# A state space layer on one Trainium2 core: how its input reaches the products for the states

## The chip, the core and the metric

The program runs on one core of one Trainium2 chip. The metric is the device time of one execution in microseconds (us), less being better. The engines of a core run side by side, each through a queue of its own in program order: TensorE (PE; its weight loads stand as PEld), VectorE (DVE), ScalarE (ACT), GpSimd (POOL) and SyncE (SP). SP computes nothing; here it issues the loads of the weights. ACT and POOL issue some transfers too.

## The reference, cut to what matters

Three blocks of a language model run one after the other on 256 places with 1024 features. The third block has a state space layer (`s5_mixer`), in which 32 groups of 16 inputs each drive 64 complex states:

```python
bu = jnp.einsum('bsgh,gph->bsgp', uf.astype(jnp.complex64), b_bar)
a = jnp.broadcast_to(lam_bar, bu.shape)
_, states = lax.associative_scan(combine, (a, bu), axis=1)
y = jnp.einsum('bsgp,ghp->bsgh', states, c).real + d_skip * uf
```

Beside it stand a short convolution and an attention with q, k and v; then an output projection and a feed-forward layer.

## The kernel before

All weights are read as 32-bit numbers and used as a high and a low part. A feeder (`Feeder`, lines 35 to 117) does this: SP loads a chunk into one of three buffers `raw` (line 61), ACT writes the high part `wh` (line 72), DVE the low part `wl` (line 86), and TensorE multiplies high by high, high by low and low by high. As soon as a chunk is split, SP is given the load that takes its buffer. Six units (half a chunk each, mostly) may be split ahead of their use. Since every engine works in program order, a unit's `wl` on DVE also stands behind whatever was issued to DVE before it.

The third block is `block2` (lines 1169 to 1359). Its order around the change:

1. `enter` makes q. The generator `s5` is then started (line 1210): POOL issues three loads, `bT`, `cT` and `dT`, from DRAM, where earlier code has left prepared matrices (line 824).
2. `fm_pair` multiplies for the first half of u (two of the four blocks of 128 features); `put_u(0)` scales it on DVE (line 1206) into `uT`, which is laid out as [128 features, block, i, k] for place 4k + i. The next `fm_pair` and `put_u(1)` do the second half.
3. A further `fm_pair` makes kv. With `tick` the generator `s5` is taken one step on, and from here it is stepped between the other products: after kv, after ks, after kw, and then in `conv_in`, in whose steps the generator `heads` (norms and transposes of q and k) takes part too.

A step J of the loop at line 887 calls `outputs(J - 2)` and then `states(J)`. There are 32 groups, 8 in each block J; two groups share one set of 128 rows of states, so a block has four sets of 32 features (jj). Four consecutive places (i) are taken together, so a step in time is four places long, and 64 such steps (k) remain for the scan.

`states(J)` (line 837) needs, for each set jj, the product of 32 features by four places with 128 states, real and imaginary (e). Before the change a product always spans all 128 rows of features. To keep the four sets apart, POOL first writes `um` (`masked`, line 830): four copies of the block of u, each with three quarters of its rows set to zero by the mask `rows4`. One product (line 842) then has 256 columns (four sets of 64), and four of them, one for each i, are added up. `masked(0)` is made by POOL right after `put_u(0)`; `masked(J + 1)` stands behind the products of block J, since there is one buffer. After the products ACT copies the sums to `bu` (line 847), and POOL (lines 852, 853, 864, 865) and DVE (lines 854 to 869) rotate, scan and rotate back.

`outputs(J)` (line 872) multiplies `uT` and the states with `dT` and `cT` and writes back over `uT`.

In the lists of instructions each of the products in 32-bit numbers stands as two matmuls.

Of the kernel before, what the change touches and what calls it, by code (L numbers as in the profile page):

```python
# [9 lines left out]
F32 = _mybir.dt.float32  # L10
# [4 lines left out]
OP = _mybir.AluOpType  # L15
# [130 lines left out]
class Net:  # L146
# [669 lines left out]
    def s5(self, p, uT, sp):  # L816

        nc = self.nc
        V, G, A, PE = nc.vector, nc.gpsimd, nc.scalar, nc.tensor
        bT = sp.tile([128, 4, 2, 4, 128], F32, name="bT")  # L820
        cT = sp.tile([128, 4, 2, 4, 128], F32, name="cT")
        dT = sp.tile([128, 4, 4, 128], F32, name="dT")
        for t, src in zip((bT, cT, dT), p["dram"]):
            G.dma_start(t, src)
        yield

        def t4(name, bufs=1):
            return sp.tile([128, 4, 64], F32, tag=name, bufs=bufs, name=name)

        def masked(J):  # L830
            um = sp.tile([128, 4, 4, 64], F32, tag="um", bufs=1, name="um")
            u2 = um.rearrange("p b i k -> p b (i k)")
            G.tensor_tensor(u2, uT[:, J].rearrange("p i k -> p (i k)")[:, None, :].to_broadcast([128, 4, S]),
                            self.rows4[:, :, None].to_broadcast([128, 4, S]), op=OP.mult)
            return um

        def states(J):

            ps = self.tr()
            for e in range(2):  # L840
                for i in range(4):
                    PE.matmul(ps[:, e * 256:e * 256 + 256], bT[:, 3 - i, e, J, :], um[0][:, :, i, :],  # L842
                              start=i == 0, stop=i == 3)
            if J < 3:
                um[0] = masked(J + 1)
            bu = sp.tile([128, 2, 4, 64], F32, tag="bu", bufs=1, name="bu")
            A.activation(bu.rearrange("p e j t -> p (e j t)"), ps, AF.Copy)
            c, s = p["sc"][:, 0, 4 * J:4 * J + 4, :], p["sc"][:, 1, 4 * J:4 * J + 4, :]
            br, bi = bu[:, 0], bu[:, 1]

            t1, t2, t3, t4_ = t4("t1"), t4("t2"), t4("t3"), t4("t4")
            G.tensor_tensor(t3, bi, c, op=OP.mult)
            G.tensor_tensor(t4_, br, s, op=OP.mult)
            V.tensor_tensor(t1, br, c, op=OP.mult)
            V.tensor_tensor(t2, bi, s, op=OP.mult)
            V.tensor_tensor(t1, t1, t2, op=OP.add)
            V.tensor_tensor(t3, t3, t4_, op=OP.subtract)
            for g in (t1, t3):
                for jj in range(4):
                    m = p["m4"][:, 4 * J + jj:4 * J + jj + 1].to_broadcast([128, 64])  # L860
                    V.tensor_tensor_scan(g[:, jj, :], m, g[:, jj, :], 0.0, op0=OP.mult, op1=OP.add)
            gr, gi = t1, t3
            hr, hi, t5, t6 = t4("hr", 2), t4("hi", 2), t4("t2"), t4("t4")
            G.tensor_tensor(hi, gr, s, op=OP.mult)
            G.tensor_tensor(t6, gi, c, op=OP.mult)
            V.tensor_tensor(hr, gr, c, op=OP.mult)
            V.tensor_tensor(t5, gi, s, op=OP.mult)
            V.tensor_tensor(hr, hr, t5, op=OP.subtract)
            V.tensor_tensor(hi, hi, t6, op=OP.add)
            return hr, hi  # L870

        def outputs(J, h):
            ps = self.tr()
            for lag in range(4):
                PE.matmul(ps[:, lag * 64:256], dT[:, lag, J, :], uT[:, J, 0:4 - lag, :].rearrange("p i k -> p (i k)"),
                          start=lag == 0, stop=False)
            for i in range(4):
                for jj in range(4):
                    sl = slice(32 * jj, 32 * jj + 32)
                    for e in range(2):  # L880
                        PE.matmul(ps[sl, i * 64 + 1:i * 64 + 64], cT[:, i, e, J, sl], h[e][:, jj, :63],
                                  start=False, stop=i == 3 and e == 1, tile_position=(0, 32 * jj))
            A.activation(uT[:, J].rearrange("p i k -> p (i k)"), ps[:, :S], AF.Copy)
        um = [masked(0)]
        yield
        h = {}
        for J in range(6):
            if J > 1:
                outputs(J - 2, h.pop(J - 2))
            if J < 4:  # L890
                h[J] = states(J)
            yield
# [276 lines left out]
    def block2(self, p, next_g):  # L1169
# [23 lines left out]
        with ExitStack() as ctx:  # L1193
# [6 lines left out]
            with ExitStack() as inner:  # L1200
                s5 = self.s5(p, uT, pool("s5", inner))

                def put_u(o, ps):

                    for a in range(2):
                        V.tensor_tensor(uT[:, 2 * o + a].rearrange("p i k -> p k i"),
                                        r3(ps)[:, a].rearrange("p (k i) -> p k i", i=4),
                                        self.rb.rearrange("p (k i) -> p k i", i=4), op=OP.mult)
                pq = self.enter(next_g)
                next(s5)  # L1210
                d["q"], d["qq"] = [], []
                for t in range(2):
                    q = self.act.tile([128, D], F32, tag="xs", bufs=2, name="q")
                    A.activation(q[:, :512], pq[t], AF.Copy, scale=self.r[:, t:t + 1])
                    d["qq"].append(q)
                    d["q"].append(q[:, :512])
                heads = self.heads(p, d, bp)
                ps = fm_pair()
                self.bcast_r()
                next(heads)  # L1220
                put_u(0, ps)
                put_u(1, fm_pair())
                next(s5)
                ps = fm_pair()
                kv = bp.tile([128, 2, S], F32, name="kv")
                self.times_r(kv.rearrange("p a t -> p (a t)"), ps)
                d["kv"] = [kv[:, i, :] for i in range(2)]
                background.append(s5)
                tick()

                def keys(name, n):
                    pk = [self.mm() for _ in range(2)]
                    self.tm([q[:, :n] for q in pk], x, KT)
                    out = []
                    for t in range(2):
                        k = bp.tile([128, n], F32, name="%s%d" % (name, t))
                        A.activation(k, pk[t][:, :n], AF.Copy, scale=self.r[:, t:t + 1])
                        out.append(k)
                    return out
                ks = keys("ks", 256)  # L1240
                tick()
                kw = keys("kw", 280)
                for name, k in (("s", ks), ("w", kw)):
                    d["k" + name] = [q[:, 0:128] for q in k]
                    d["v" + name] = [q[:, 128:256] for q in k]
                d["gates"] = [q[:, 256:280] for q in kw]
                tick()
                next(heads)
                background.append(heads)

                rb2 = bp.tile([128, S], F32, name="rb2")
                V.tensor_tensor(rb2, self.rb, self.rb, op=OP.mult)

                def conv_in(n):
                    cx = ring()
                    V.tensor_tensor(r3(cx), r3(fm_pair()), rb2[:, None, :].to_broadcast([128, 2, S]), op=OP.mult)
                    tick(n)
                    V.tensor_tensor(cx, cx, fm_pair(), op=OP.mult)
                    tick(n)
                    pb = fm_pair()  # L1260
                    tick(n)
                    return cx, pb
                cx, pb = conv_in(1)
                for g in (s5, heads):
                    for _ in g:
                        pass
                background.clear()
# [158 lines left out]
    def consts2(self):  # L1426
# [9 lines left out]
        for h in range(2):  # L1436
# [16 lines left out]

        self.both = c.tile([32, 16], F32, name="both")
        G.tensor_tensor(self.both, self.ident[0:32, 0:16], self.ident[0:32, 16:32], op=OP.add)

        self.rows4 = c.tile([128, 4], F32, name="rows4")
        G.memset(self.rows4, 1.0)
        G.affine_select(self.rows4, self.rows4, pattern=[[-32, 4]], compare_op=OP.is_ge, fill=0.0, base=0,
                        channel_multiplier=1)  # L1460
        G.affine_select(self.rows4, self.rows4, pattern=[[32, 4]], compare_op=OP.is_ge, fill=0.0, base=31,
                        channel_multiplier=-1)
        self.cmask = c.tile([128, 2, 8], F32, name="cmask")
        G.memset(self.cmask, 0.0)
        G.affine_select(self.cmask, self.cmask, pattern=[[128, 2], [-32, 8]], compare_op=OP.is_ge, fill=-1e30,
# [403 lines left out]
```

## Time and profile before

| | |
|---|---|
| median of 3 runs | 1514.34 us (1512.48 to 1516.26) |
| the profiled execution | 1515.93 us, its span 1514.2 us |
| TensorE busy | 1455.3 us, 96% of the span |
| VectorE busy | 1058.6 us, 70% |
| ScalarE busy | 803.9 us, 53% |
| GpSimd busy | 223.4 us, 15% |
| mean granted clock of TensorE | 0.982 |

The span goes from the first to the last instruction of the program on the core. Lines such as L86 are lines of the kernel. A row of a timeline gives start, duration, engine, line, operation, what is written and read, shapes, the count of merged instructions, and in brackets how long the engine sat idle before and what ended it. The end of a matmul is modelled, so a busy TensorE may still have room. [...]

### The profile page before, as it was taken

Reading aid. Unit: us, or ns where it says so; the run is one execution under the profiler, and the core shown is the slowest. Engines: PE = TensorE matmul, PEld = TensorE weight load, DVE = VectorE, ACT = ScalarE, POOL = GpSimd, SP = SyncE. Lnnn points to the kernel's source line nnn. Section 1 sums busy time; section 2 is a strip of 40 time slices with the busy share of each in tenths; the row PEclk is TensorE's granted clock in tenths of the full one; section 3 lists DMA queues with packets and bytes.
Section 4 is the critical chain, followed back from the end, with each engine's and each line's share of the span. In section 5 each row is a group of like instructions: output and inputs, shape, how many; then the busy total and the mean of one; then the engine's idle time right before and its main releaser. Section 6 shows DMA issues by size and latency. Waiting matters only on the chain.

```text
span 1514.2 us, 23224 instructions
## 1 busy us (share of the span) xinstructions
PE 1455.3 (96%) x9185; PEld 1289.3 (85%) x9185; DVE 1058.6 (70%) x1776; ACT 803.9 (53%) x1319; POOL 223.4 (15%) x267
## 2 busy tenths in 40 slices
PE   8999997899999999999889998999999999999999
PEld 7888887878888888888887997889898899888887
DVE  6777476877774777746687778757976656677753
ACT  6665357566554556545756434545355544465541
POOL 1200000000000040000000455601426444000000
PEclk9999999899999999999989999999999999999999
DMA  8656643346555575564443836767345445555562
GB/s 291 189 176 204 205 139 113 124 132 217 194 181 198 167 236 168 185 217 130 125 137 104 261 119 211 235 223 256 109 130 182 126 135 186 167 188 189 180 208 70
DMA packets 212893, 265.27 MB, mean 175 GB/s; under 512 B 6120, under 2 KB 175568, under 8 KB 212400
## 3 DMA queue, kind: packets, MB, share of 16 engines
q1 hardware_dynamic: 208224, 250.64, 51.0%
q0 software_dynamic: 3232, 9.86, 2.0%
q10 hardware_dynamic: 1328, 3.29, 0.6%
q8 instruction: 72, 1.18, 0.3%
q14 instruction: 37, 0.30, 0.1%
HBM read 257.47 MB, written 6.29 MB: 174 GB/s over the span
## 4 chain that ended last, share of the span: by engine, by line
PE 72%; DVE 16%; ACT 6%; issue 4%; POOL 1%; DMA 1%; SPq 0%; ACTq 0%; DVEq 0%; POOLq 0%
PE mm L201 25%; PE mm L187 17%; PE mm L185 10%; DVE wl L86 5%; PE mm L164 5%; PE mm L166 5%; PE mm L165 5%; PE mm L184 2%; ACT wh L72 2%; DVE xc L1407 1%; ACT xx L341 1%; DVE xx L343 1%; POOL wl L86 0%; DVE bw L755 0%; PE tr L842 0%
## 5 line engine op out<-in xcount | busy, mean ns | idle before, releaser
L86 DVE TENSOR_TENSOR wl<-raw,wh 128x1024 fp32r<-128x1024 f32 (+1 forms) x441 | 546.3, 1252 | 263.2 <-ACT wh L72 260.1
L72 ACT ACTIVATE wh<-raw 128x1024 fp32r<-128x1024 f32 (+2 forms) x472 | 483.2, 1048 | 174.6 <-PE mm L201 112.8
L187 PE MATMUL mm<-xx,wh 128*128 128x512 f32 x1120 | 399.1, 396 | 0.0
L185 PE MATMUL mm<-xx,wl 128*128 128x256 f32 x1280 | 330.7, 279 | 0.0
L164 PE MATMUL mm<-xx,wh 128*128 128x256 f32 x864 | 253.2, 293 | 2.9 <-ACT wh L72 2.9
L185 PEld LDWEIGHTS mm<-xx,wl 128*128 128x128 f32 x1280 | 241.2, 188 | 13.8
L166 PE MATMUL mm<-xx,wl 128*128 128x256 f32 x864 | 249.4, 289 | 2.4 <-DVE wl L86 2.4
L165 PE MATMUL mm<-xx,wh 128*128 128x256 f32 x864 | 249.1, 288 | 0.0
L187 PEld LDWEIGHTS mm<-xx,wh 128*128 128x128 f32 x1120 | 210.1, 188 | 43.2
L164 PEld LDWEIGHTS mm<-xx,wh 128*128 128x128 f32 x864 | 171.1, 198 | 4.0 <-ACT wh L72 3.3
L166 PEld LDWEIGHTS mm<-xx,wl 128*128 128x128 f32 x864 | 170.4, 197 | 3.1 <-DVE wl L86 3.1
L165 PEld LDWEIGHTS mm<-xx,wh 128*128 128x128 f32 x864 | 170.7, 198 | 0.3
L201 PE MATMUL mm<-wl,hh 128*128 128x512 f32 x440 | 137.7, 394 | 0.0
L201 PE MATMUL mm<-wh,hh 128*128 128x512 f32 x440 | 137.3, 393 | 0.0
L201 PE MATMUL mm<-wh,hl 128*128 128x512 f32 x440 | 137.3, 393 | 0.0
L201 PEld LDWEIGHTS mm<-wl,hh 128*128 128x128 f32 x440 | 82.7, 188 | 18.7
L201 PEld LDWEIGHTS mm<-wh,hl 128*128 128x128 f32 x440 | 82.7, 188 | 18.5
L201 PEld LDWEIGHTS mm<-wh,hh 128*128 128x128 f32 x440 | 82.3, 188 | 18.8
L201 PE MATMUL mm<-wh,xx 128*128 128x512 f32 (+3 forms) x384 | 93.7, 377 | 0.3 <-DVE xx L343 0.3
L86 POOL TENSOR_TENSOR wl<-raw,wh 128x1024 fp32r<-128x1024 f32 x31 | 78.1, 2534 | 80.5 <-ACT wh L72 80.5
L585 ACT ACTIVATE sg<-sg 128x512 f32<-128x512 f32 x50 | 31.6, 632 | 107.4 <-DVE sg L419 107.4
L201 PEld LDWEIGHTS mm<-wh,xx 128*128 128x128 f32 x384 | 70.2, 194 | 12.2 <-DVE xx L343 1.2
(674 smaller groups left out, 1913.5 us busy)
## 6 DMA issues: line engine op xcount, KB each, us to landing
raw<-ffn_w_gu SPq DMA_DIRECT2D x80, 1024.0 KB, 5.2
raw<-ffn_w_down SPq DMA_DIRECT2D x50, 1024.0 KB, 5.1
raw<-w_in SPq DMA_DIRECT2D x24, 1024.0 KB, 5.1
raw<-ffn_w_gate_up SPq DMA_DIRECT2D x20, 1024.0 KB, 5.1
raw<-mix_w_in SPq DMA_DIRECT2D x10, 1024.0 KB, 5.5
raw<-mix_w_out SPq DMA_DIRECT2D x8, 1024.0 KB, 4.9
raw<-ffn_w_gu SPq DMA_DIRECT2D x14, 512.0 KB, 5.1
raw<-ffn_w_down SPq DMA_DIRECT2D x10, 512.0 KB, 3.7
```

Of the source, the lines that this page charges most:

```text
L72: nc.scalar.activation(h, raw, AF.Copy)
L86: v.tensor_tensor(l, raw, h.bitcast(F32), op=OP.subtract)
L164: mm(ps, a[0], b[0], start=start, stop=False)
L165: mm(ps, a[0], b[1], start=False, stop=False)
L166: mm(ps, a[1], b[0], start=False, stop=stop)
L184: nc.tensor.matmul(p, wh[:, k, :], self.xx[:, k, :], start=True, stop=False)
L185: nc.tensor.matmul(p[:, :S], wl[:, k, :], self.xh[:, k, :], start=False, stop=False)
L187: nc.tensor.matmul(p, wh[:, k, :], self.xx[:, k, :], start=False, stop=k == nk - 1)
L201: self.nc.tensor.matmul(ps, x[a][:, k, ts], w[b][:, i, :], start=k == 0 and a + b == 0, stop=k == nk - 1 and b == 1)
L341: nc.scalar.activation(self.xh[:, k, ts], p, AF.Copy, scale=g[:, k:k + 1])
L343: nc.vector.scalar_tensor_tensor(self.xl[:, k, ts], p, g[:, k:k + 1], self.xh[:, k, ts].bitcast(F32), op0=OP.mult, op1=OP.subtract)
L585: nc.scalar.activation(sg, sg, AF.Silu)
```

## The change

`masked`, `um` and the mask `rows4` go. The contraction of a product for the states now spans 32 features of one set and the four places i at once: `u4` holds in rows 32i to 32i + 31 the features of set jj at places 4k + i. So a product has 64 columns, needs no adding up, and there are again eight of them in a block. `u4` is brought into this order by SP: for each half of u, 16 transfers from SBUF to SBUF, each of 32 rows with two pieces of 64 numbers (16 KB). `bT` is loaded to match, in four transfers of 32 rows instead of one of 128. The 16 transfers of a half are issued by a step of the generator right after the `put_u` of that half, so one more step stands behind `put_u(0)`.

```diff
         bT = sp.tile([128, 4, 2, 4, 128], F32, name="bT")
+        u4 = sp.tile([128, 4, 4, 64], F32, name="u4")
...
-        for t, src in zip((bT, cT, dT), p["dram"]):
+        for i in range(4):
+            G.dma_start(bT[32 * i:32 * i + 32].rearrange("f j e J n -> f j (e J n)"),
+                        p["dram"][0][:, 3 - i].rearrange("(j f) e J n -> f j (e J n)", j=4))
+        for t, src in zip((cT, dT), p["dram"][1:]):
             G.dma_start(t, src)
         yield
+        for o in range(2):
+            for i in range(4):
+                for jj in range(4):
+                    nc.sync.dma_start(u4[32 * i:32 * i + 32, 2 * o:2 * o + 2, jj, :],
+                                      uT[32 * jj:32 * jj + 32, 2 * o:2 * o + 2, i, :])
+            yield
...
-        def masked(J):
-            um = sp.tile([128, 4, 4, 64], F32, tag="um", bufs=1, name="um")
-            u2 = um.rearrange("p b i k -> p b (i k)")
-            G.tensor_tensor(u2, uT[:, J].rearrange("p i k -> p (i k)")[:, None, :].to_broadcast([128, 4, S]),
-                            self.rows4[:, :, None].to_broadcast([128, 4, S]), op=OP.mult)
-            return um
...
             ps = self.tr()
             for e in range(2):
-                for i in range(4):
-                    PE.matmul(ps[:, e * 256:e * 256 + 256], bT[:, 3 - i, e, J, :], um[0][:, :, i, :],
-                              start=i == 0, stop=i == 3)
-            if J < 3:
-                um[0] = masked(J + 1)
+                for jj in range(4):
+                    c = e * 256 + jj * 64
+                    PE.matmul(ps[:, c:c + 64], bT[:, jj, e, J, :], u4[:, J, jj, :], start=True, stop=True)
...
-        um = [masked(0)]
-        yield
         h = {}
...
                 put_u(0, ps)
+                next(s5)
                 put_u(1, fm_pair())
                 next(s5)
...
-        self.rows4 = c.tile([128, 4], F32, name="rows4")
-        G.memset(self.rows4, 1.0)
-        G.affine_select(self.rows4, self.rows4, pattern=[[-32, 4]], compare_op=OP.is_ge, fill=0.0, base=0,
-                        channel_multiplier=1)
-        G.affine_select(self.rows4, self.rows4, pattern=[[32, 4]], compare_op=OP.is_ge, fill=0.0, base=31,
-                        channel_multiplier=-1)
```

## Rows read from the trace of the kernel before

**Rows 1.** The page: the chain that ended last, by engine

```profile
PE 72%; DVE 16%; ACT 6%; issue 4%; POOL 1%; DMA 1%; SPq 0%; ACTq 0%; DVEq 0%; POOLq 0%
```

**Rows 2.** Stretches of 4 us: busy time (instructions) of PE, PEld, DVE, ACT, POOL; clock; DMA

```profile
1048.00:1052.00 4.00, 4.00 (x35) 4.00 (x34) 2.80 (x5) 3.89 (x7) 0.00 (x0) 1.00 0.53 152
1052.00:1056.00 4.00, 4.00 (x32) 3.87 (x31) 4.00 (x5) 1.11 (x2) 1.89 (x1) 1.00 0.00 0
...
1088.00:1092.00 4.00, 3.41 (x16) 2.66 (x14) 3.38 (x13) 2.12 (x6) 0.38 (x1) 1.00 0.00 0
1092.00:1096.00 4.00, 1.60 (x11) 1.10 (x11) 3.90 (x13) 2.54 (x5) 1.94 (x2) 0.97 0.00 0
1096.00:1100.00 4.00, 4.00 (x23) 4.00 (x23) 3.97 (x7) 2.42 (x3) 0.00 (x0) 0.60 0.27 73
```

**Rows 3.** Timeline, TensorE after the last product for the states

```profile
1093.56 1.23 PE L945 MATMUL tr<-ident,q 128*128 128x128 f32 x8 [2.15 <-DVE q L929]
```

**Rows 4.** Timeline, VectorE, from put_u(0) to the end of block J = 2

```profile
1045.60 2.36 DVE L86 TENSOR_TENSOR wl<-raw,wh 128x1024 fp32r<-128x1024 f32 x2 [4.20 <-ACT wh L72]
...
1051.54 1.10 DVE L1206 TENSOR_TENSOR uT<-mm,rb 128x256 f32<-128x256 f32 x2
...
1059.21 1.59 DVE L854 TENSOR_TENSOR t<-bu,sc 128x256 f32<-128x256 f32 x1 [0.55 <-ACT bu L847]
...
1061.72 0.85 DVE L856 TENSOR_TENSOR t<-t,t 128x256 f32<-128x256 f32 x1
...
1068.55 2.12 DVE L854 TENSOR_TENSOR t<-bu,sc 128x256 f32<-128x256 f32 x1
...
1076.64 6.32 DVE L86 TENSOR_TENSOR wl<-raw,wh 128x1024 fp32r<-128x1024 f32 x4
1082.89 0.96 DVE L854 TENSOR_TENSOR t<-bu,sc 128x256 f32<-128x256 f32 x1
...
1084.76 0.42 DVE L856 TENSOR_TENSOR t<-t,t 128x256 f32<-128x256 f32 x1
...
1089.38 0.47 DVE L915 TENSOR_REDUCE ss<-junk 128x2 f32<-128x128 f32 x2
```

**Rows 5.** Timeline, ScalarE: the load waits, rb, and the first bu

```profile
1044.51 2.01 ACT L72 ACTIVATE wh<-raw 128x1024 fp32r<-128x1024 f32 x2 [5.72 <-DMA raw<-w_in]
1048.11 1.06 ACT L72 ACTIVATE wh<-raw 128x1024 fp32r<-128x1024 f32 x1 [1.60 <-DMA raw<-w_in]
1049.08 0.37 ACT L415 ACTIVATE rb<-tr 128x256 f32<-128x256 f32 x1
...
1058.58 0.60 ACT L847 ACTIVATE bu<-tr 128x512 f32<-128x512 f32 x1 [5.47 <-issue]
```

**Rows 6.** Timeline, TensorE: products for the states, and 64-column products elsewhere

```profile
1054.88 3.61 PE L842 MATMUL tr<-um,bT 128*128 128x256 f32 x16
...
290.39 1.45 PE L1738 MATMUL tr<-xdt,E 128*128 128x64 f32 x12
291.65 0.48 PE L164 MATMUL mm<-wh,yh 128*128 128x512 f32 x1
```

**Rows 7.** The masked copies on POOL (ns min/median/max)

```profile
L833 POOL TENSOR_TENSOR um<-uT,rows x4: 1887/1961/2610, 1052.2 to 1079.9; 128x1024 f32<-128x1024 f32 x4
```

**Rows 8.** Transfers by line: ns of one issue (min/median/max), or KB and us to landing

```profile
L61 SPq DMA_DIRECT2D raw<-w_in x26: 367/368/368, 1000.8 to 1257.7; - x26
...
out_dram<-x SPq DMA_DIRECT2D x3, 256.0 KB, 2.0
...
g1raw<-ffn_pre_g ACTq DMA_DIRECT2D x1, 8.0 KB, 3.2
...
bT<-dram_b POOLq DMA_DIRECT2D x1, 2048.0 KB, 8.5
```

**Rows 9.** Timeline, POOL: the eighth and ninth transfer of a series

```profile
35.42 0.52 POOL L313 DMA_DIRECT2D prow<-ssd_conv_b  x1
37.66 0.53 POOL L313 DMA_DIRECT2D prow<-ssd_conv_w  x1 [1.72 <-DMA prow<-mix_pre_g]
```

## Prediction

> **What bounds the kernel now.** I read the chain of waits first. TensorE holds 72% of it and VectorE 16% [rows 1]: over the whole run, time is won by taking work from TensorE or by ending its waits. That is an average, though, and the change sits in some 45 us of the span. So I next read that place in stretches of 4 us. The reader is to see two things [rows 2]. Up to about 1088 us TensorE is busy all the time, but so is VectorE from 1052 on. Then TensorE falls to 3.41 and 1.60 us of 4, while VectorE stays near 4, and after that the granted clock is 0.60 for a stretch. TensorE has run out of work that VectorE has made ready. The row of the wait says the same: the transposes of q, at 1093.56, come after a wait for a DVE result [rows 3].
>
> So between put_u(0) and the transposes of q the later of two queues decides, and today that is VectorE's. I therefore follow VectorE in order of time [rows 4]. It does put_u(0) (ending at 1051.54 + 1.10 = 1052.64), weight splits, put_u(1), then the block of states(0), more splits, states(1), four splits, states(2), and at 1089.38 the first norm that the transposes hang on. All stands in program order; a split never overtakes a block of states that is late. The block of states(0) starts when ACT has written the first bu: 1058.58 + 0.60 = 1059.18 [rows 5]. From there to 1089.38 VectorE needs 30.2 us, nearly without a pause. What the change is worth is read from these two: when the first bu comes, and how long the 30.2 us become.
>
> **Part 1, the products.** Before, 16 matmuls of 256 columns take 3.61 us a block. Products of 64 columns with a full set of weights stand elsewhere in the kernel: twelve from 290.39 to the next matmul at 291.65, 105 ns each, 1.45 us with the last one's tail [rows 6]. Sixteen would take 1.45 + 4 x 0.105 = 1.87 us. That is 1.74 us less a block, 7.0 us in four. All of it lies on TensorE ahead of the transposes of q, where TensorE waits for VectorE at the end; by itself it lengthens that wait and is worth nothing. [...]
>
> **Part 2, the masked copies.** Four copies of about 2 us on POOL go [rows 7]. VectorE instructions beside them are longer than the same ones elsewhere [rows 4]: line 854 takes 1.59 and 2.12 us with a copy beside it, 0.96 without (0.63 + 1.16 saved); four splits take 6.32 us, against 2.36 for two undisturbed (6.32 - 2 x 2.36 = 1.60 saved); line 856 waits in the slowed pair at 0.85 instead of 0.42, in two blocks (0.86 saved). Sum 4.2 us of the 30.2, leaving 26.0. The first copy's gain falls ahead of the first bu, where VectorE will wait anyway, and the mask's three small set-up instructions are long past: nothing for either.
>
> **Part 3, the transfers of u.** This is the new wait. The first product of states(0) needs all 16 transfers of the first half, and they can't be issued before put_u(0) ends at 1052.64. SP needs 0.37 us for one issue, whatever its size in these rows [rows 8]; with the check of a semaphore I take 0.39, and 0.52 (POOL's pace [rows 9]) as the upper end. The last is issued 15 x 0.39 = 5.9 us later, at 1058.5. To land it takes 2.0 us by the nearest row in kind (a store of SP's with the engines to itself) and 3.2 by the smallest in size (8 KB) [rows 8]; I take 2.0, since it too starts on quiet engines. POOL's ninth transfer in a row waited until the first had landed [rows 9], so eight seem to be open at a time; at 8 x 0.39 = 3.1 us that doesn't bind here until landing takes longer. So TensorE, which stands ready at 1054.88 [rows 6], starts at 1060.5 (ends: 1060.2 to 1063.6), after 5.6 us without work.
>
> Before, 3 us without work in 8 brought the granted clock to 0.60 over the next stretch [rows 2]. Here the idle time is longer, so I price the first block at 1.2 GHz: 1.87 + 16 x 0.105 = 3.6 us (lower end 1.87). From the last product to bu it is 1059.18 - 1054.88 - 3.61 = 0.7 us. The first bu is there at 1060.5 + 3.6 + 0.7 = 1064.8, 5.6 us later than before. After that TensorE keeps ahead of VectorE: its three blocks are shorter and VectorE still has 26.0 us to do.
>
> Behind the waiting SP stand weight loads: one after each group of 16. They start some 6 and 12 us late (twice 16 x 0.39). Six units, three pairs of products, are split ahead of their use, and TensorE itself comes 5.6 us later, so I cost this at nothing; without that cover each microsecond that a unit is late is one on TensorE. ACT, which waits in order for those loads, has nothing urgent behind them that isn't late by as much. The second group has until states(2), two pairs of products later. ACT's writes over uT come later still, and the added step of the generator moves nothing else: `tick` finds the loop over J where it found it before.
>
> **Part 4, bT in four pieces.** Three more issues on POOL, 1.6 us [rows 9], before cT and dT; POOL has nothing else due. But the loads share the DMA engines with the weight loads for which ACT waits 5.72 and 1.60 us, and behind the second wait stands rb, behind that put_u(0) [rows 5]. So what delays these loads delays Part 3 one for one. No row shows a load to 32 rows. Lower end: no change. Upper end: half the pace. bT landed after 8.5 us, of which 2.0 are any transfer's [rows 8], so 6.5 us more; from 1048 to 1052 the DMA engines were only 0.53 busy, which takes back 1.9 [rows 2]: 4.6 us. I take 1.0, near the lower end, as every load in the rows goes at an undivided pace. [...]
>
> **The sum.** First bu 5.6 us later, bT 1.0, less 4.2 for the copies: 2.4 us longer. The profiled execution took 1515.93 us (span 1514.2), 1.6 above the median of the runs, 1514.34; so 1518.3 against its own time and 1516.7 against the median. A measurement of this kernel can tell about 0.3%, 4.5 us, from no change, so this is no change.
>
> **Rivals.** First, faster: the transfers hide, or the pace of issue for 16 KB is far quicker than 0.37 us. If u were in place by 1054.88, the first bu would come at 1054.88 + 1.87 + 0.7 = 1057.4, 1.8 us earlier than before; with the 4.2 that is 6.0 us less, 1508.3. It counts as faster from a first bu at about 1058.9. For it: the work does fall on all three engines, and nothing else is on the DMA engines between 1052 and 1056 [rows 2]. Against it: the constant 0.37 us over 26 loads.
>
> Second, slower: bT's pieces move at about half pace and hold back the loads in front of rb. Then put_u(0) is 3 to 4.6 us late rather than 1.0; with the other terms (5.6 - 4.2 = 1.4) that is 4.4 to 6.0 us longer, about 1519.5. It decides once put_u(0) ends after 1055.7. For it: ACT is already waiting for these loads with the DMA engines full. Against it: the stretch after 1048, which is half empty.
>
> Third, TensorE's 7.0 us arrive in full (1507.3), as the share of 72% would suggest. Against it stands the wait at 1093.56; it would need VectorE not to be the last there. I count it into the faster case.
>
> **How the numbers follow.** Forecast (within 4.5 us of no change) 0.58; slower 0.30, nearly all of it the second rival, some of it a landing of 3.2 us with an issue of 0.52; faster 0.12. The range starts from my term's ends: at full clock and with no delay by bT it is 5.6 - 1.7 - 4.2 = -0.3, and at the slow ends of Part 3 (3.1 later) plus half of bT's bound it is 1.4 + 3.1 + 2.3 = 6.8. It goes on to 1511, half way to the first rival, and 1522, past the second.
>
> **What would show it.** Right: VectorE idle for several us before its first line 854; the last of the first 16 landing near 1060.5; TensorE idle from about 1054.9 with a granted clock near 0.5 after it; line 842 at about 105 ns apart at full clock; 26 us from the first bu to the norm of k; a longer wait at the transposes of q. Wrong: issues under 0.2 us apart, line 842 without idle time before it, rb more than 3 us later, or TensorE waiting for a weight unit between the keys and the first conv product.

## The result, and the profile after

The changed kernel takes 1525.93 us (median of 3 runs, 1525.9 to 1526.78) against 1514.34: 1.0078 times the time before, 95% interval [1.0065, 1.0092]. It is 11.6 us slower, outside the predicted range and on the side of the second rival, beyond its price. Two of the executions further down, one of e7 and one of e12, took some 5003 us; the ratios leave them out.

The profiled execution has a span of 1524.8 us. I compare from one fixed point, the issue of the first of the raw weight loads that rb waits for, the raw load from here on (1031.08 before, 1031.54 after), so that what varies earlier in a run drops out. In us behind that issue:

| | put_u(0) ends | first bu read | norm L915 | end of span |
|---|---|---|---|---|
| before | 21.56 | 28.13 | 58.30 | 483.1 |
| after | 26.37 | 41.28 | 68.07 | 493.3 |
| change of each step | +4.8 | +8.3 | -3.4 | +0.4 |

Each change is that of the step alone: first bu minus put_u(0) is 14.91 us against 6.57, norm minus first bu 26.79 against 30.17. They sum to 10.2 us, of 10.85 between the two profiled executions (1526.78 against 1515.93) and 11.6 between the medians; the rest is not located.

The chain of waits of the changed kernel over this stretch (start, length, what) tells the story in the order of time:

```profile
1039.63 13.68 DMA raw<-w_in
...
1056.83 1.09 DVE uT L1206 x2
1058.04 0.75 SPq L834
1058.84 0.59 SPq L834
...
1065.24 0.59 SPq L834
1065.88 1.80 DMA u<-uT
1067.67 0.45 issue
1068.13 3.98 PE tr L847 x16
```

Two rows of the chain are waits that add up: a weight load of 13.68 us in front of put_u(0), then issues of SP at 0.64 us spacing, one behind the other. That load was issued just after the last of bT's pieces had landed (1039.37; bT before: 1034.04), and what lay ahead of it was late by as much: the raw load of 1031.54 landed after 18.8 us, 13.4 before. The stretches of 4 us there (columns as in [rows 2]), first in the kernel before:

```profile
1028.00:1032.00 4.00, 3.76 (x21) 2.90 (x19) 3.31 (x8) 1.57 (x7) 1.46 (x3) 1.00 1.00 418
1032.00:1036.00 4.00, 4.00 (x19) 3.29 (x18) 3.11 (x10) 4.00 (x8) 0.00 (x0) 1.00 0.97 413
```

And in the changed kernel:

```profile
1028.00:1032.00 4.00, 3.75 (x21) 3.03 (x20) 3.30 (x8) 1.11 (x5) 3.33 (x7) 1.00 0.98 219
1032.00:1036.00 4.00, 4.00 (x19) 3.14 (x18) 3.09 (x9) 4.00 (x10) 0.00 (x0) 1.00 1.05 219
...
1064.00:1068.00 4.00, 0.00 (x0) 0.00 (x0) 0.00 (x0) 0.00 (x0) 0.00 (x0) 0.70 0.13 27
1068.00:1072.00 4.00, 3.87 (x17) 3.73 (x17) 0.00 (x0) 0.00 (x0) 0.00 (x0) 0.50 0.61 172
```

The reader is to see two things. In the first two rows the DMA engines are busy all the time (0.98, 1.05), as before, and yet move 219 GB/s instead of 418 and 413. From 1064 to 1068 no engine computes anything: everything waits for transfers that keep the DMA engines 0.13 busy. That is a queue of issues, not of bytes.

ScalarE's waits, to be held against [rows 5]:

```profile
1050.36 2.01 ACT L72 ACTIVATE wh<-raw 128x1024 fp32r<-128x1024 f32 x2 [11.11 <-DMA raw<-w_in]
1053.41 1.06 ACT L72 ACTIVATE wh<-raw 128x1024 fp32r<-128x1024 f32 x1 [1.04 <-DMA raw<-w_in]
1054.37 0.36 ACT L415 ACTIVATE rb<-tr 128x256 f32<-128x256 f32 x1
...
1072.19 0.60 ACT L849 ACTIVATE bu<-tr 128x512 f32<-128x512 f32 x1 [13.79 <-PE tr L847]
```

VectorE, against [rows 4] (lines 856 and 858 are 854 and 856 of before):

```profile
1056.83 1.08 DVE L1206 TENSOR_TENSOR uT<-mm,rb 128x256 f32<-128x256 f32 x2
...
1072.82 0.43 DVE L856 TENSOR_TENSOR t<-bu,sc 128x256 f32<-128x256 f32 x1 [10.40 <-ACT bu L849]
...
1074.16 0.84 DVE L858 TENSOR_TENSOR t<-t,t 128x256 f32<-128x256 f32 x1
...
1082.14 0.43 DVE L856 TENSOR_TENSOR t<-bu,sc 128x256 f32<-128x256 f32 x1 [1.05 <-ACT bu L849]
...
1083.49 0.84 DVE L858 TENSOR_TENSOR t<-t,t 128x256 f32<-128x256 f32 x1
...
1088.56 4.62 DVE L86 TENSOR_TENSOR wl<-raw,wh 128x1024 fp32r<-128x1024 f32 x4
...
1099.61 0.47 DVE L915 TENSOR_REDUCE ss<-junk 128x2 f32<-128x128 f32 x2
```

TensorE's products, against [rows 6], and then all its waits from 1046 to 1106 (us in total, times, longest), against [rows 3]:

```profile
1068.13 3.98 PE L847 MATMUL tr<-u,bT 128*128 128x64 f32 x16 [6.98 <-DMA u<-uT]
1079.44 1.89 PE L847 MATMUL tr<-u,bT 128*128 128x64 f32 x16
```

```profile
PE tr L847 <- DMA u<-uT: 7.0, 1, 7.0
PE tr L945 <- DVE q L929: 2.1, 1, 2.1
PE mm L164 <- ACT wh L72: 1.7, 1, 1.7
PE mm L166 <- DVE wl L86: 0.8, 1, 0.8
```

The second block at 1.89 us is half of the 3.61 of before: what the change was made for is there. The wait at the transposes of q is as long as before (2.1 against 2.15), so VectorE still decides that end; what the shorter products are worth comes out in e7 and e13. All is shifted by what happens before 1072.82.

Last, SP's issues by line (ns, minimum, median, maximum), against [rows 8]:

```profile
L834 SPq DMA_DIRECT2D u<-uT x32: 587/595/1072, 1058.0 to 1079.5; - x32
```

### The profile page after: what moved, and what is told of

Its sections match the earlier page's. It is cut to its first block, busy times and chain, and to the rows that moved or that the text cites. A ratio compares the mean times of both kernels' runs of the same rounds, so it can differ in the third digit from the quotient of the medians.

```text
span 1524.8 us, 23282 instructions
## 1 busy us (share of the span) xinstructions
PE 1456.2 (95%) x9185; PEld 1291.1 (85%) x9185; DVE 1051.1 (69%) x1776; ACT 804.0 (53%) x1319; POOL 215.7 (14%) x263
## 4 chain that ended last, share of the span: by engine, by line
PE 72%; DVE 14%; ACT 6%; issue 4%; POOL 2%; DMA 1%; SPq 1%; ACTq 0%; DVEq 0%; POOLq 0%
PE mm L201 25%; PE mm L187 17%; PE mm L185 10%; PE mm L164 5%; DVE wl L86 5%; PE mm L166 5%; PE mm L165 5%; PE mm L184 2%; ACT wh L72 2%; POOL wl L86 1%; DMA raw<-w_in 1%; ACT xx L341 1%; DVE xc L1408 1%; PE tr L330 1%; SPq L834 0%
```

## The experiments

The theory has parts. A: bT's pieces of 32 rows move at half pace and make put_u(0) late. B: sixteen issues on one queue make the first bu late. C: without the masked copies VectorE needs some 4 us less. A, B and C lie one behind the other. The main rivals are that the lateness comes from something else around it, and that C came from the shorter products.

All runs, in us behind the raw load's issue as above, with the median time and its ratio to the kernel before (whose medians beside them were 1514.45 to 1515.44):

| run | put_u(0) | first bu | norm | end | median | ratio, 95% interval |
|---|---|---|---|---|---|---|
| e1 before, bT in pieces | 26.05 | 32.05 | 62.21 | 486.8 | 1517.75 | 1.0021 [1.0012, 1.0030] |
| e2 bT whole | 21.73 | 36.57 | 62.55 | 487.5 | 1521.80 | 1.0053 [1.0040, 1.0066] |
| e3 one transfer | 26.48 | 32.63 | 58.54 | 483.5 | 1514.35 | 0.9998 [0.9989, 1.0006] |
| e4 joined rows | 26.30 | 40.94 | 67.87 | 492.9 | 1524.62 | 1.0067 [1.0055, 1.0079] |
| e5 engine copies | 21.62 | 32.22 | 57.49 | 480.5 | 1516.30 | 1.0010 [1.0000, 1.0020] |
| e6 two queues | 26.26 | 45.31 | 70.60 | 495.8 | 1527.61 | 1.0085 [1.0072, 1.0098] |
| e7 before, block copies | 21.62 | 28.15 | 55.90 | 479.5 | 1510.97 | 0.9970 [0.9960, 0.9981] |
| e8 whole and one transfer | 21.55 | 27.30 | 53.04 | 478.1 | 1514.20 | 0.9985 [0.9976, 0.9994] |
| e9 spread rows | 22.17 | 37.33 | 64.26 | 489.4 | 1521.32 | 1.0044 [1.0031, 1.0056] |
| e10 order through DRAM | 22.08 | 32.14 | 58.23 | 483.1 | 1514.21 | 1.0000 [0.9992, 1.0009] |
| e11 e7 again | 21.64 | 28.13 | 55.88 | 479.4 | 1510.10 | 0.9969 [0.9958, 0.9981] |
| e12 before, small stores | 21.69 | 28.12 | 58.28 | 484.3 | 1517.19 | 1.0012 [1.0002, 1.0023] |
| e13 e8 without small stores | 22.17 | 27.57 | 53.30 | 476.4 | 1509.14 | 0.9961 [0.9949, 0.9972] |

**A: bT's pieces (e1, e2, e9).** First the pieces alone, in the kernel before:

```diff
-        for t, src in zip((bT, cT, dT), p["dram"]):
+        for i in range(4):
+            G.dma_start(bT[32 * i:32 * i + 32], p["dram"][0][32 * i:32 * i + 32])
+        for t, src in zip((cT, dT), p["dram"][1:]):
```

> The kernel before, with the one edit that bT is loaded in four pieces of 32 rows. Theory A (the pieces move at about half pace, hold back the raw weight loads in front of rb, and so put_u(0)): put_u(0) ends 4 to 5 us later than before (1052.64), the stretch after 1028 shows about 219 GB/s as in the changed kernel instead of 418, and the run is 3 to 5 us longer than before, about 1518.5. Rival (the late put_u(0) of the changed kernel comes from something else, such as the code around it or SP's order): put_u(0) within 1 us of before and a time within 1.5 us of before.

The pieces alone make put_u(0) 4.5 us late (26.05 against 21.56) and the run 3.2 us longer by the ratio (1.8 to 4.5). Theory A. Two stretches of this run:

```profile
1028.00:1032.00 4.00, 3.76 (x21) 2.93 (x20) 3.34 (x10) 3.41 (x11) 1.46 (x3) 1.00 0.97 205
1032.00:1036.00 4.00, 4.00 (x22) 3.42 (x21) 2.97 (x12) 3.90 (x5) 0.00 (x0) 1.00 1.00 240
```

Then the reverse, in the changed kernel (and the load of bT as before):

```diff
-                A.dma_start(db[0][:, q - 1], stg)
+                for j in range(4):
+                    A.dma_start(db[0][32 * (4 - q):32 * (4 - q) + 32, j], stg[32 * j:32 * j + 32])
```

> The changed kernel, with the copy of b stored in DRAM in the order of the new rows, so that bT comes in one load of 128 rows. Theory A: bT moves at about 415 GB/s again, rb and put_u(0) end about 4.8 us earlier than in the changed kernel, the first bu too, and the time falls by 4 to 5 us, to about 1521. Rival: put_u(0) or the time within 1.5 us of the changed kernel. The 16 smaller stores that take the place of four lie far earlier and should cost nothing.

put_u(0) is back at 21.73 and the time falls by 4.1 us. One sentence of mine here was wrong, that the smaller stores cost nothing; e12 takes it up.

Is it the size of a piece, or where its rows lie? This edit changes only the latter (and the rows of `u4` with it, as the products need):

```diff
-            G.dma_start(bT[32 * i:32 * i + 32].rearrange("f j e J n -> f j (e J n)"),
+            G.dma_start(bT[i::4].rearrange("f j e J n -> f j (e J n)"),
...
-                    nc.sync.dma_start(u4[32 * i:32 * i + 32, 2 * o:2 * o + 2, jj, :],
+                    nc.sync.dma_start(u4[i::4, 2 * o:2 * o + 2, jj, :],
...
```

> The changed kernel, with the rows of bT and of the ordered u in another order: piece i goes to rows i, i + 4, i + 8 and so on (32 rows spread over all 128) instead of rows 32 i to 32 i + 31. Sizes, counts and order of all transfers stay. Theory A1 (half pace belongs to 32 rows that lie together): the stretch in which bT's pieces move shows about 415 GB/s instead of 219, put_u(0) ends about 21.7 us behind the issue of the raw load in front of it instead of 26.4, as with bT in one load, and the time falls by 5 to 6 us, to about 1520 (the whole load gave back some 3 us on ScalarE's queue by its twelve extra stores, which are not here). Theory A2 (half pace belongs to pieces of 32 rows, wherever they lie, or to four transfers in place of one): 219 GB/s and 26.4 us as before, time within 1.5 us of 1525.9.

The same four pieces, with the same bytes and number of rows, on rows that are four apart:

```profile
1028.00:1032.00 4.00, 3.76 (x21) 3.02 (x20) 3.31 (x7) 1.41 (x6) 2.97 (x6) 1.00 0.99 355
1032.00:1036.00 4.00, 4.00 (x19) 3.15 (x18) 3.14 (x10) 4.00 (x8) 0.00 (x0) 1.00 1.08 454
```

355 and 454 GB/s instead of 219 (the second row has some of the next load in it), put_u(0) at 22.17, 4.6 us off the time by the medians. The pieces landed about 1.3 us apart instead of 2.5. A1 holds: what costs is that the 32 rows lie together, 205 to 240 GB/s in e1 and the changed kernel against 355 to 454 here. Why neighbouring rows go at about half the pace no trace shows.

**B: the issues of u (e3, e4, e6).** One transfer for each half:

```diff
-            for i in range(4):
-                for jj in range(4):
-                    nc.sync.dma_start(u4[32 * i:32 * i + 32, 2 * o:2 * o + 2, jj, :],
-                                      uT[32 * jj:32 * jj + 32, 2 * o:2 * o + 2, i, :])
+            nc.sync.dma_start(u4[:, 2 * o:2 * o + 2], uT[:, 2 * o:2 * o + 2])
```

> The changed kernel, with one transfer of 128 rows for each half of u instead of sixteen; rows and features of u stay in their old order, so the products for the states are made of u in another order. Theory B (the first bu waits for 16 issues on SP at 0.64 us each, one after another): the last landing moves from 11.7 us behind put_u(0) to about 2.5, the first bu comes about 9 to 10 us earlier than in the changed kernel, and the time falls by 8 to 10 us, to about 1517 (put_u(0) is still late by bT's pieces). Rival (the landing or the half clock of the products holds it up, not the number of issues): the last landing still 6 us or more behind put_u(0), and less than 4 us won.

The transfer, issued at 1054.36, lands at 1056.82, 2.6 us behind put_u(0) instead of 11.7. The first bu comes 8.65 us earlier (32.63 against 41.28) and the end of the span 9.8. By the medians it is 11.6 us, more than I expected. Theory B. Part of the gain is the clock's: the first block took 2.71 us here (granted clock 0.75 from 1056 to 1060), 3.98 in the changed kernel (0.50 from 1068 to 1072).

What sets the 0.64 us? First the length of the pieces. Two runs of 256 bytes become one of 512:

```diff
-            uT = bp.tile([128, 4, 4, 64], F32, name="uT")
+            uT = bp.tile([128, 2, 4, 2, 64], F32, name="uT")
...
+                    nc.sync.dma_start(u4[32 * i:32 * i + 32, o, jj],
+                                      uT[32 * jj:32 * jj + 32, o, i])
...
```

> The changed kernel, with u and its ordered copy laid out so that each of the 32 transfers moves 32 runs of 512 bytes instead of 64 of 256; all else is the same. Theory B1 (the pace of issue, 0.64 us, hangs on the number of pieces): issues near 0.37 us like those of the weight loads, last landing 7.5 to 8 us behind put_u(0) instead of 11.7, time about 4 us less, 1522. Theory B2 (the pace is one of transfers of 32 rows, or from SBUF to SBUF, whatever their pieces): issues stay near 0.6 us and the time within 1.5 us of 1525.9.

```profile
L834 SPq DMA_DIRECT2D u<-uT x32: 532/589/951, 1056.1 to 1077.2; - x32
```

589 ns against 595: B2. Halving the number of pieces changes nothing that counts. Which part of B2 holds, the 32 rows or SBUF to SBUF, stays open: e3's two transfers of 128 rows were issued in 0.54 and 0.47 us, between the two. Then two queues:

```diff
-                    nc.sync.dma_start(u4[32 * i:32 * i + 32, 2 * o:2 * o + 2, jj, :],
+                    (nc.sync if jj % 2 else A).dma_start(u4[32 * i:32 * i + 32, 2 * o:2 * o + 2, jj, :],
...
```

> The changed kernel with half of the sixteen issues of each half of u on SP and half on ScalarE's queue. Theory B (issues are made one after another on a queue, at about 0.64 us): the last landing comes 8 x 0.64 + 1.8 = about 7 us behind put_u(0) instead of 11.7, the first bu 4.5 to 5 us earlier than in the changed kernel, and the time falls by 4 to 5 us, to about 1521. Rival (something the queues share sets the pace, so that two queues issue at 1.28 us each): last landing still 11 to 12 us behind, time within 1.5 us of 1525.9.

The local number is right: the last of the first sixteen landed 6.9 us behind put_u(0). The time is wrong by 6.6 us, and this miss taught most. ScalarE's rows:

```profile
1056.74 5.29 ACTq L834 DMA_DIRECT2D u<-uT  x8
1062.07 1.62 ACT L72 ACTIVATE wh<-raw 128x1024 fp32r<-128x1024 f32 x2 [7.54 <-DMA u<-uT]
1066.03 7.01 ACTq L834 DMA_DIRECT2D u<-uT  x8
1073.09 1.23 ACT L72 ACTIVATE wh<-raw 128x560 fp32r<-128x560 f32 x2 [9.40 <-DMA u<-uT]
1074.23 0.58 ACT L849 ACTIVATE bu<-tr 128x512 f32<-128x512 f32 x1
```

The engine that issues is held for each issue. ScalarE computes nothing for 7.54 us: its queue waits for put_u(0) and then makes eight issues in 5.29 us, and the weight splits stand behind them. The splits delay put_u(1) (it ends 35.60 behind the raw load, 29.06 in the changed kernel), and the second eight, which wait for put_u(1), stand in ScalarE's order ahead of the copy of the first bu. These took 7.01 us. Eight transfers of the two queues were open by then, the first of them a weight load that SP had issued at 1064.41; SP issued nothing from 1067.3 to 1071.48, just after that load had landed (6.7 us from its issue). TensorE had ended those products at 1066.70; bu was copied at 1074.23. The wait had only moved to another queue.

**C: the masked copies (e7, e11).** The kernel before, with the masked tile set to zero once and only its blocks that are not zero written:

```diff
...
-            G.tensor_tensor(u2, uT[:, J].rearrange("p i k -> p (i k)")[:, None, :].to_broadcast([128, 4, S]),
-                            self.rows4[:, :, None].to_broadcast([128, 4, S]), op=OP.mult)
+            for jj in range(4):
+                sl = slice(32 * jj, 32 * jj + 32)
+                A.activation(um[sl, jj], uT[sl, J], AF.Copy)
...
```

> The kernel before, with its mask written otherwise: the masked tile is set to zero once and ScalarE copies only the four blocks of 32 rows that are not zero (256 elements a row instead of 1024 on GpSimd); products, order of rows and bT's load as before. Theory C (GpSimd's copies lengthen VectorE's instructions beside them by about 4 us in all): from the first bu to the first norm 26 to 27 us instead of 30.2, the first bu within 1 us of before, and the time 3 to 4.5 us shorter than before, about 1511. Rival (the shorter stretch of the changed kernel came from its shorter products): still about 30 us, and a time within 1.5 us of before.

From first bu to norm it is 27.75 us against 30.17, with the long products still in place. In that stretch VectorE now also waits for bu:

```profile
1066.05 0.43 DVE L854 TENSOR_TENSOR t<-bu,sc 128x256 f32<-128x256 f32 x1 [0.85 <-ACT bu L845]
...
1072.45 4.62 DVE L86 TENSOR_TENSOR wl<-raw,wh 128x1024 fp32r<-128x1024 f32 x4
1078.13 0.43 DVE L854 TENSOR_TENSOR t<-bu,sc 128x256 f32<-128x256 f32 x1 [1.05 <-ACT bu L845]
```

27.75 - 0.85 - 1.05 = 25.85, the 26.0 of the prediction; the four splits take 4.62 us as in the changed kernel, against 6.32 in [rows 4]. So the gain belongs to the missing copies on GpSimd; the rival, that it came from the shorter products, fails. The run is 4.5 us shorter than before by the ratio (2.9 to 6.1).

The two waits say something that I had not expected: ScalarE had those bu late because TensorE ended its long products late.

```profile
1065.42 0.60 ACT L845 ACTIVATE bu<-tr 128x512 f32<-128x512 f32 x1 [3.11 <-PE tr L842]
...
1077.50 0.60 ACT L845 ACTIVATE bu<-tr 128x512 f32<-128x512 f32 x1 [3.37 <-PE tr L842]
```

In e13 below, which has the short products and no masked copies either, the same two instructions of VectorE start without a wait, and the stretch is 25.7 us:

```profile
1065.05 0.96 DVE L852 TENSOR_TENSOR t<-bu,sc 128x256 f32<-128x256 f32 x1
...
1076.11 0.96 DVE L852 TENSOR_TENSOR t<-bu,sc 128x256 f32<-128x256 f32 x1
```

So the two engines are nearly level here: once the copies are gone, the short products are worth about 2 us by these rows.

**Do they add? (e5, e8, e10, e12, e13).** Sixteen small copies a half on three engines, with bT whole:

```diff
...
+                    dst = u4[32 * i:32 * i + 32, 2 * o:2 * o + 2, jj, :]
+                    src = uT[32 * jj:32 * jj + 32, 2 * o:2 * o + 2, i, :]
+                    if n % 3 == 0:
+                        A.activation(dst, src, AF.Copy)
+                    elif n % 3 == 1:
+                        G.tensor_copy(dst, src)
+                    else:
+                        V.tensor_copy(dst, src)
...
```

> The changed kernel with bT in one load (as in the second experiment) and with u brought in order by sixteen small copies a half on ScalarE, GpSimd and VectorE in turn, 32 rows to 32 other rows, in place of the transfers. Theory A+B (both delays in front of the first bu are gone, the gain from the missing masked copies stays): the last copy ends 2 to 3 us behind put_u(0), the first bu comes at or before the time of the kernel before, and the run is 3 to 5 us shorter than before, 1510 to 1512. Rival (the small copies cost VectorE as much as the masked copies did, or TensorE is not held up by VectorE here): within 1.5 us of before, or 7 us shorter.

The copies ended 2 us behind put_u(0), as expected, but the first bu came 4.1 us later than in the kernel before: ScalarE's six copies of the second half (1061.76, 1.91 us) wait for put_u(1) and stand ahead of the first bu in its order, as in e6. And from the raw load on the run is 2.6 us shorter than before, yet the whole run is not. The same showed with the edits of e2 and e3 together:

> The second and the third experiment together: the changed kernel with bT in one load and one transfer of 128 rows for each half of u (rows and features of u stay in their old order, so the products for the states are made of u in another order). If the two delays are serial, as theory says, their gains add: 1525.9 - 4.1 - 11.5 = about 1510.3. Rival (they overlap, or another wait comes up): no more than 1.5 us below the third experiment, about 1513.

4.9 us shorter than before from the raw load on, 2.3 by the ratio (0.9 to 3.6), and the raw load itself issued at 1034.81 (1027.75 to 1032.18 in the runs that have bT's four stores as they were). So the twelve extra stores were tried alone, in the kernel before:

```diff
-                A.dma_start(db[0][:, q - 1], stg)
+                for j in range(4):
+                    A.dma_start(db[0][32 * j:32 * j + 32, q - 1], stg[32 * j:32 * j + 32])
```

> The kernel before, with each of the four stores of b's copy to DRAM issued as four stores of 32 rows on ScalarE's queue; nothing else. Theory D (twelve more issues at about 0.5 us each stand in ScalarE's order in front of the copies that TensorE waits for): TensorE falls from 11.5 us of busy time to about 9.7 in the 12 us from 944 on, and the run is 2.5 to 4.5 us longer than before, about 1518. Rival (the stores cost nothing, the difference was chance between runs): within 1.5 us of before.

```profile
945.92 0.63 PE L774 MATMUL tr<-ident,bw 128*128 128x128 f32 x4 [0.68 <-DVE bw L755]
948.34 1.16 PE L784 MATMUL tr<-cw,bw 128*32 128x32 f32 x64 [1.78 <-ACT dd L788]
```

TensorE waits 1.78 us at 948.34 for a copy that stands behind the stores on ScalarE, and is busy 9.35 of the 12 us from 944 instead of 11.51, at a granted clock of 0.72. The run is 1.8 us longer by the ratio (0.3 to 3.5), less than I said but not nothing. Theory D, at a smaller size. TensorE's wait at that place stands in all four runs with the extra stores (1.64 to 1.78 us in e2, e5, e8 and e12) and in no other. What it costs differs: the granted clock over those 12 us was 0.72 in the profiles of e8 and e12 and 1.00 in that of e2. So do the times, 1509.7 to 1515.3 in e8 and 1515.1 to 1521.1 in e12; both profiles come from the upper part of these ranges. Then both repairs without those stores:

```diff
-                A.dma_start(db[0][:, q - 1], stg)
+                A.dma_start(db[0][:, 4 - q], stg)
...
+        G.dma_start(bT.rearrange("p j e J n -> p j (e J n)"), p["dram"][0].rearrange("(j f) i e J n -> (f i) j (e J n)", j=4))
...
+            nc.sync.dma_start(u4[:, o], uT[:, o])
```

> The changed kernel with the row order feature-then-place, bT in one load out of the four stores as they were, and one direct transfer of 128 rows for each half of u (rows and features of u stay in their old order, so the products for the states are made of u in another order). Theory (the two gains add, and the extra stores had hidden it): first bu about 27.3 us behind the raw load's issue as in the eighth experiment, no loss between 944 and 956, and 1509.5 to 1511. Rival (the gains overlap): 1513 to 1515 again.

1509.14 us, 0.4 below the range that adding gave: the delays A and B are serial and C stays. As its u stands in another order than the products need, e13, like e3 and e8, is a measurement and no version to keep. With the same load of bT, u is brought in order by a store to DRAM and one load back:

```diff
+            nc.sync.dma_start(p["dram"][3][o], uT[:, o])
+            nc.sync.dma_start(u4[:, o].rearrange("p j a k -> p j (a k)"), p["dram"][3][o].rearrange("(j f) i a k -> (f i) j (a k)", j=4))
```

> The changed kernel with the row order feature-then-place, so that bT is one load of 128 rows out of stores that stay as they were, and u is brought in order by two transfers a half (one store to DRAM, one load of 128 rows) instead of sixteen. Theory (A, B and C serial, and the twelve extra stores of the whole load were what kept the earlier combination from its gain): put_u(0) at 21.6 us behind the raw load's issue, the load of u landing about 5 us behind put_u(0), the first bu some 1.5 us later than before, 26 us from there to the first norm, and 1511 to 1512.5 in all. Rival (the stores on ScalarE's queue cost nothing and the missing 4 us lie elsewhere): about 1515.

The load landed 5.1 us behind put_u(0), as expected, and bu to norm took 26.1 us. The time didn't follow, since I had left out the clock: the first block came after a wait of 3.85 us and ran at half clock (granted 0.50 from 1056 to 1060).

```profile
1056.82 3.65 PE L844 MATMUL tr<-u,bT 128*128 128x64 f32 x16 [3.85 <-DMA u<-dram_u]
```

So the first bu is 4.0 us later than before, not 1.5, and C's 4.1 are used up. The time is nearer to the rival's 1515, but the stores are not the cause, as e10 has no extra ones.

> The seventh experiment's kernel once more, beside the tenth's on the same chip: which of the two is the better version. Theory: 1511, ratio to before about 0.997, and within 1.5 us of the tenth's, since its first bu comes 1.5 us earlier and its four copies a block on ScalarE cost VectorE up to 1 us of waiting for bu. Rival (its gain was that chip's): within 1.5 us of before.

1510.10 us, 0.9969 [0.9958, 0.9981]: the kernel before with block copies beats both kernels, each time it was run.

## Why the prediction was wrong

The mechanism was right in the main: VectorE decides from the first bu on, the first bu becomes late, and what the masked copies give back is less. Two terms of the sum were too small, and they carry the miss.

**Part 4, bT in four pieces: taken as 1.0 us, measured 4.8.** The step that failed is "I take 1.0, near the lower end, as every load in the rows goes at an undivided pace". Every large load in those rows went to 128 rows; none bore on 32. With no row in the trace, I let rows of another kind decide between the ends. The half pace of the upper end was my estimate, which no row of the kernel before shows; the runs then showed it, 205 to 240 GB/s in e1 and the changed kernel against 413 and 418 before. The upper end, 4.6, was right, and so was the mechanism of the second rival, with its sign: rb came 4.8 us later. Its price of 1519.5 was too low mainly because it took Part 3 as I had it.

**Part 3, the issues: taken as 0.39 us each, measured 0.64 from one to the next.** "SP needs 0.37 us for one issue, whatever its size in these rows" rested on 26 loads that are each issued alone. The trace of before had issues one directly behind another:

```profile
L61 SPq DMA_DIRECT2D raw<-ssm_w_glu x8: 367/434/502, 1139.1 to 1178.5; - x8
```

These come in pairs (0.92 us for two at 1139.10): 0.37 for the first, 0.50 for the one behind it. That row was nearer in kind than the one I used. At 0.64, fifteen spacings are 9.6 us; with 0.1 to start, 0.16 more for the first issue and 1.8 for landing (2.0 predicted) that is the 11.7 measured, 3.8 over the prediction. Of this, 1.5 came back, since the first product needs only thirteen of the sixteen transfers, not all as I had said, and TensorE began at 1068.13, before the last landed at 1069.60; 0.4 went again, as the first block took longer.

**Part 1** held in its size: 1.89 us a block (1.87); the 105 ns of the row were right. That it is worth nothing was said of the kernel before, and no run has short products beside the masked copies. Without the copies it is worth about 2 us (e7 against e13). The longer wait at the transposes of q didn't come (2.1 us); it was 2.7 in e8 and e13, whose first block took 1.97 us and not 3.98.

**Part 2** held as a sum: 26.8 us from first bu to norm (26.0), or 25.7 without the wait of 1.05 us for the second bu, and e7 shows its cause. Against "TensorE keeps ahead of VectorE" stands that wait: the granted clock was still 0.52 from 1072 to 1076. In the terms there was luck: line 854 gave 1.16 and 1.69 us (0.63 and 1.16 predicted) and the four splits 1.70 (1.60), but line 856 gave nothing, as it still takes 0.84 in the first two blocks (0.86 predicted for both).

The half clock of the first block held in kind: the granted clock was 0.50 from 1068 to 1072, and the block took 3.98 us (3.6 predicted), some of it waits for the last transfers. The 1.2 GHz of that price no run shows; they show the granted clock only as a share. The weight loads behind SP cost TensorE nothing, as predicted: its four waits from 1046 to 1106 hold none for a unit after 1053.

The sum as predicted was 1.0 + 5.6 - 4.2 = 2.4; as measured 4.8 + 8.3 - 3.4 + 0.4 = 10.2. The range failed with its bounds: I ended it at half of bT's bound and at an issue of 0.52, and added no case in which both terms are at their slow ends. That case is 1.4 + 3.1 + 4.6 = 9.1 us, 1523.4, still short of what came.

## What to carry to other kernels

Price a run of issues by rows of issues that follow one another, and count them as work of the engine that makes them: sixteen small transfers on a wait cost 10 us of queue here while the DMA engines were 0.13 busy. When a layout is free, let a transfer's rows spread over all 128 and not fill 32 neighbours; here that was worth 4.6 us for an index. Where two engines are nearly level, relieve both: the missing copies gave their full worth only with the shorter products. And where the trace has no row for an operation, keep the full range of the bound: rows of another kind don't choose between its ends.

## What was not expected of the hardware

- The same four transfers of 512 KB landed about 2.5 us apart on 32 neighbouring rows (some 210 GB/s) and about 1.3 us apart on 32 rows four apart (some 410 GB/s); from issue to landing, 5.9 to 11.7 us became 4.6 to 6.7.
- An issue from SBUF to SBUF took 0.59 us in a row of them, with runs of 256 or 512 bytes alike (medians 595 and 589 ns); a weight load directly behind one took 0.52 to 0.53 instead of 0.37.
- Issues on two queues at once kept the pace of each (e6, medians 596 and 607 ns) as long as the transfers landed soon. With eight open on the two together, neither made a further one until the oldest had landed (SP none from 1067.3 to 1071.48), as POOL alone in [rows 9] (1.72 us idle before its ninth) and SP alone in the changed kernel: behind a weight load of 1068.50 and seven transfers of u, its ninth went out at 1073.89, as that load landed (5.4 us), and its issue took 1.07 us. What sets the eight is not shown.
- A copy from 32 rows to 32 other rows took about 0.3 us for 128 elements a row on ScalarE and VectorE alike (e5: six in 1.95 us, five in 1.46).
